# A log-sum-exp over rows whose input is laid out in three pieces instead of two

## The chip, the cores and the metric

The kernel runs on one core of a Trainium2 chip. The metric is the device time of one execution in microseconds, as the median of several runs; a profile of one execution shows the span from its first to its last instruction.

## The reference

```
def setup_inputs():
    batch, seq, dim = 32, 512, 1024
    return {"x": np.random.randn(batch, seq, dim).astype(np.float32)}

def reference(x):
    max_x = np.max(x, axis=-1, keepdims=True)
    return (max_x.squeeze(-1) + np.log(np.sum(np.exp(x - max_x), axis=-1))).astype(np.float32)
```

There are 32 x 512 = 16384 rows of 1024 float32 numbers (67.1 MB in), and one number comes out for each row.

## The kernel before

The 16384 rows are spread over 128 partitions, 128 rows to each. The first 128 x 112 rows of the input form one piece, in which each partition owns 112 consecutive rows (448 KB); the last 128 x 16 rows form the second, in which each partition owns 16 (64 KB). A load takes a stretch of columns of one piece: the same stretch for all partitions, so its 128 parts lie one partition's share apart in memory.

The list LOADS gives 18 loads in order, each with its size in rows and what is done with it. All are issued by SP (L139) into a ring of 48 rows in SBUF. A load is placed behind the one before; if it does not fit ahead of the ring's end, it begins at the ring's start again. Before SP issues a load it waits for every engine step that still reads the ring rows the load will overwrite (the list `users`), and only for these.

The kernel computes exp without subtracting the maximum first, then sums, then takes the Ln. ACT does the exponentials in place (L228) as soon as a load has landed, in the order of the list. The letters say who does the sums:

- R: DVE sums whole rows (L239), so many rows in one instruction.
- F: POOL adds the second half of each row to the first (L233), and DVE sums the halves later (`reduce_folded`, L171). DVE does this behind the next R or T group, or ahead of the next F group.
- T: DVE folds and sums one row with one instruction (L249).
- Y and Z: the last row in two parts, which ACT itself sums (L202).

If a load ends inside a row, ACT also exponentiates the part that has landed. The T rows and the last one are in the small loads at the end, whose sizes fall from 4.46875 rows to 0.46875. When 119 rows are summed, ACT takes the Ln of all rows of the first piece (L268) and SP stores them (L276). At the end ACT takes the Ln of the other 16 rows (L279, L281) and SP stores them (L285). Beside this, DVE and PE check that no sum left the range in which exp without the maximum is safe (L146 to L308); a branch that redoes the work with the maximum follows if the check fails, and is not taken with this input. SP issues load 0 ahead of the start barrier (`start_early`).

The lines that fix the layout and the sizes are:

```
LOADS = [
    (16, "R16"), (16, "R16"), (16, "R16"), (16, "F9 R7"), (13.5, "F6 R7"), (12.5, "R7 F6"),
    (9, "R5 F4"), (7, "F4 R3"), (6, "F2 F2 R2"), (4.46875, "T4"), (3.25, "T3"), (2.46875, "T3"),
    (1.8125, "T2"), (1.3125, "T1"), (0.96875, "T1"), (0.71875, "T1"), (0.53125, "Y"), (0.46875, "Z"),
]
```

Of the kernel before, what the change touches and what calls it, by code (L numbers as in the profile page):

```python
# [13 lines left out]
CEILING = 27.0  # L14
STEEP = 2.0**48
RING = 48
B = 16
LATE = 119

LOADS = [
# [3 lines left out]
]  # L27

# [24 lines left out]
def kernel(  # L53
# [5 lines left out]
    nc = tc.nc  # L59
# [4 lines left out]
    P = nc.NUM_PARTITIONS  # L64
# [6 lines left out]
    x_flat = x.flatten_outer_dims()  # L71
    n, d = x_flat.shape
    assert n % P == 0
    NC = n // P
    H = d // 2
    W = NC - B
    LAST = NC - 1
    x_rows = x_flat[0 : P * W].rearrange("(p c) d -> p (c d)", p=P)
    x_rest = x_flat[P * W : n].rearrange("(p c) d -> p (c d)", p=P)
    out_flat = out.rearrange("a b -> (a b)")  # L80
    out_rows = out_flat[0 : P * W].rearrange("(p c) -> p c", p=P)
    out_rest = out_flat[P * W : n].rearrange("(p c) -> p c", p=P)

    def source(e0, size):
        assert e0 >= W * d or e0 + size <= W * d
        return x_rest[:, e0 - W * d : e0 - W * d + size] if e0 >= W * d else x_rows[:, e0 : e0 + size]

    loads = [
        (int(size * d), [(op[0], 0 if op[0] == "Y" else int(op[1:] or 1)) for op in ops.split()])
# [5 lines left out]
    def sbuf(name, cols, dtype=fp32, rows=P):  # L95
        return nc.alloc_sbuf_tensor(name, [rows, cols], dtype).ap()
# [3 lines left out]
    res = sbuf("res", NC)  # L100
# [18 lines left out]
    sp = Counted(nc, nc.sync, "early_store")  # L119
    done = nc.alloc_semaphore("done")  # L120
    again = nc.alloc_semaphore("again")
    ready = nc.alloc_semaphore("ready")
    stored = nc.alloc_semaphore("stored")
# [10 lines left out]
    def load(i, here, done_before, size):  # L134
        for a, b, who, at in users:
            if a < here + size and b > here:
                sp.wait(who, at)
        users[:] = [u for u in users if not (u[0] < here + size and u[1] > here)]
        return nc.sync.dma_start(  # L139
            out=ring[:, here : here + size], in_=source(done_before, size)  # L140
        ).then_inc(landed[i], 16)
# [36 lines left out]
    c = 0  # L178
    p = 0
# [6 lines left out]
    for i, (size, ops) in enumerate(loads):  # L186
        if here + size > RING * d:
            assert here == p
            p = here = 0
# [7 lines left out]
        for k, (how, s) in enumerate(ops):  # L197
            rows = ring[:, p : p + s * d].rearrange("p (c d) -> p c d", d=d)
            if how in "YZ":
# [3 lines left out]
                    out=last_exp[:, here - p : end - p], in_=ring[:, here:end], func=AF.Exp,  # L203
# [10 lines left out]
            elif how == "A":  # L214
# [3 lines left out]
                    out=v, in_=v, func=AF.Exp, accum_out=sumexp[:, c : c + 1]  # L218
# [11 lines left out]
            if how == "F":  # L230
# [3 lines left out]
                    out=rows[:, :, 0:H], in0=rows[:, :, 0:H], in1=rows[:, :, H:d], op=ALU.add  # L234
                ))
                folded.append((c, s, p, at))
            elif how == "R":
                dve.wait(act, at)
                who = (dve, dve.did(nc.vector.reduce_sum(  # L239
                    out=sumexp[:, c : c + s], in_=rows, axis=AX.X  # L240
                )))
                users.append((p, p + s * d, *who))
            elif how == "T":
# [3 lines left out]
                for r in range(s):  # L247
                    lo = rows[:, r, 0:H]
                    who = (dve, dve.did(nc.vector.scalar_tensor_tensor(  # L249
                        out=lo, in0=lo, scalar=1.0, in1=rows[:, r, H:d],  # L250
# [13 lines left out]
            if c == LATE:  # L264
# [4 lines left out]
                    out=res[:, 0:W], in_=sumexp[:, 0:W], func=AF.Ln  # L269
# [3 lines left out]
                early_act = summed_by_act  # L273
        assert here == end
    sp.wait(act, ln_early)
    nc.sync.dma_start(out=out_rows, in_=res[:, 0:W]).then_inc(sp.sem, 16)  # L276

    act.wait(dve, dve.n)
    act.did(nc.scalar.activation(out=res[:, W:LAST], in_=sumexp[:, W:LAST], func=AF.Ln))  # L279
# [2 lines left out]
        out=res[:, LAST:NC], in_=last_sum, func=AF.Ln, bias=sumexp[:, LAST:NC]  # L282
    ))
    sp.wait(act, ln_last)
    nc.sync.dma_start(out=out_rest, in_=res[:, W:NC]).then_inc(stored, 16)  # L285

# [4 lines left out]
        out=clamped[:, LATE:NC], in0=sumexp[:, LATE:NC], scalar=LOW,  # L291
# [10 lines left out]
        out=over[:, 0:half], in0=last_piece[:, 0:half], scalar=CEILING,  # L302
# [15 lines left out]
            read.then_inc(done, 1)  # L318
    with nc.If(all_fine < 1):

        nc.scalar.wait_ge(sp.sem, 16)
        nc.scalar.wait_ge(stored, 16)
        rows = 0
        steps = 0
        for c0 in range(0, NC, RING):
            s = min(RING, NC - c0)
            v = ring[:, 0 : s * d].rearrange("p (c d) -> p c d", d=d)
            neg = clamped[:, c0 : c0 + s]
            if c0:
                nc.scalar.wait_ge(ready, steps)  # L330
            edge = max(c0, min(W, c0 + s))
            for c1, c2 in ((c0, edge), (edge, c0 + s)):
                if c1 == c2:
                    continue
                nc.scalar.dma_start(
                    out=ring[:, (c1 - c0) * d : (c2 - c0) * d],
                    in_=source(c1 * d, (c2 - c1) * d),
                ).then_inc(again, 16)
                rows += 16
            nc.vector.wait_ge(again, rows)  # L340
            nc.vector.tensor_reduce(
                out=neg, in_=v, op=ALU.max, axis=AX.X, negate=True
            ).then_inc(ready, 1)
            nc.vector.wait_ge(ready, steps + 1)
            nc.vector.tensor_add(
                out=v, in0=v, in1=neg[:, :, None].to_broadcast([P, s, d])
            ).then_inc(ready, 1)
            nc.scalar.wait_ge(ready, steps + 2)
            nc.scalar.activation(out=v, in_=v, func=AF.Exp).then_inc(ready, 1)
            nc.vector.wait_ge(ready, steps + 3)  # L350
            nc.vector.reduce_sum(
                out=sumexp[:, c0 : c0 + s], in_=v, axis=AX.X
            ).then_inc(ready, 1)
            steps += 4
        nc.scalar.wait_ge(ready, steps)
        nc.scalar.activation(out=res, in_=sumexp[:, 0:NC], func=AF.Ln).then_inc(ready, 1)
        nc.vector.wait_ge(ready, steps + 1)
        nc.vector.tensor_sub(out=res, in0=res, in1=clamped).then_inc(ready, 1)
        nc.scalar.wait_ge(ready, steps + 2)
        nc.scalar.dma_start(out=out_rest, in_=res[:, W:NC]).then_inc(again, 16)  # L360
        nc.scalar.dma_start(out=out_rows, in_=res[:, 0:W]).then_inc(again, 16)
        nc.scalar.wait_ge(again, rows + 32)

    nc.scalar.sem_inc(done, 1)
    nc.sync.wait_ge(done, 2)
    nc.sync.wait_ge(sp.sem, 16)
    nc.sync.sem_clear(range(landed[0].num, stored.num))
    kind = dict(sync_type="semaphore", id=stored.num, ant_name="stored")
    nc.sync.add_instruction(mybir.InstEventSemaphore(
# [53 lines left out]
```

## Time and profile before

| | us |
|---|---|
| median of 3 runs | 161.56 (161.54 to 161.56) |
| span of the profiled execution | 160.4 |
| median of the runs less that span | 1.2 |
| ACT busy, DVE busy, POOL busy | 114.5, 114.3, 37.3 |
| input moved, mean rate | 67.1 MB, 419 GB/s |

No time of the profiled execution is listed beside its span; the times of the three runs are of other executions. The busy times are sums over the whole span. A load's time "to landing" counts from its issue by SP to the moment when all its parts are there, and it includes the time for which it lies in the queue behind earlier loads. In the timeline, a bracket at the end of a row gives the idle time ahead of the instruction and what ended it.

### The profile page before, as it was taken

Reading aid. Unit: us, or ns where it says so; the run is one execution under the profiler, and the core shown is the slowest. Engines: PE = TensorE matmul, PEld = TensorE weight load, DVE = VectorE, ACT = ScalarE, POOL = GpSimd, SP = SyncE. Lnnn points to the kernel's source line nnn. Section 1 sums busy time; section 2 is a strip of 40 time slices with the busy share of each in tenths; the row PEclk is TensorE's granted clock in tenths of the full one; section 3 lists DMA queues with packets and bytes.
Section 4 is the critical chain, followed back from the end, with each engine's and each line's share of the span. In section 5 each row is a group of like instructions: output and inputs, shape, how many; then the busy total and the mean of one; then the engine's idle time right before and its main releaser. Section 6 shows DMA issues by size and latency. Waiting matters only on the chain.

```text
span 160.4 us, 219 instructions
## 1 busy us (share of the span) xinstructions
PE 2.2 (1%) x26; PEld 1.1 (1%) x26; DVE 114.3 (71%) x59; ACT 114.5 (71%) x31; POOL 37.3 (23%) x11
## 2 busy tenths in 40 slices
PE   0000000000000000000000000000000000000022
PEld 0000000000000000000000000000000000000011
DVE  0000000009999499994999859959999999999996
ACT  3000059990699708995099949991999989799996
POOL 0000000000000000000000994690004969891000
DMA  7996996996996996996999999999999999999992
GB/s 262 523 523 262 523 523 262 523 507 278 523 490 294 523 490 294 523 490 294 482 441 441 441 425 409 409 409 480 432 395 417 450 416 398 448 411 424 412 413 95
DMA packets 2881, 67.18 MB, mean 419 GB/s; under 512 B 576, under 2 KB 704, under 8 KB 1344
## 3 DMA queue, kind: packets, MB, share of 16 engines
q1 hardware_dynamic: 2880, 67.18, 97.7%
q14 instruction: 1, 0.01, 0.0%
HBM read 67.11 MB, written 0.07 MB: 419 GB/s over the span
## 4 chain that ended last, share of the span: by engine, by line
DMA 52%; ACT 28%; DVE 19%; issue 1%; PE 0%
DMA ring<-in_x_dram 52%; ACT ring L228 27%; DVE sumexp L239 15%; DVE sumexp L171 2%; DVE ring L249 1%; DVE over L301 0%; PE count L306 0%; ACT res L268 0%; DVE clamped L290 0%; DVE fine L308 0%; DVE sumexp L212 0%
## 5 line engine op out<-in xcount | busy, mean ns | idle before, releaser
L228 ACT ACTIVATE ring<-ring 128x16384 f32<-128x16384 f32 (+16 forms) x23 | 111.7, 4908 | 43.0 <-DMA ring<-in_x_dram 43.0
L239 DVE TENSOR_REDUCE sumexp<-ring 128x16 f32<-128x16384 f32 (+4 forms) x9 | 85.6, 9513 | 42.7 <-ACT ring L228 42.7
L233 POOL TENSOR_TENSOR ring<-ring 128x3072 f32<-128x3072 f32 (+3 forms) x7 | 37.1, 5313 | 107.3 <-ACT ring L228 107.3
L171 DVE TENSOR_REDUCE sumexp<-ring 128x6 f32<-128x3072 f32 (+3 forms) x7 | 18.4, 2656 | 0.0
L249 DVE SCALAR_TENSOR_TENSOR ring<-ring 128x512 f32<-128x512 f32 x15 | 9.6, 687 | 0.4 <-ACT ring L228 0.4
L125 ACT ACT_TABLE_LOAD x1 | 1.3, 1283 | 1.4 <-PEq L62 1.4
L156 PE MATMUL count<-far,bad 128*1 128x1 f32 x2 | 0.2, 164 | 153.2 <-DVE clamped L151 153.2
L160 PE MATMUL count<-sumexp,ones 128*1 128x1 f32 x18 | 1.6, 164 | 3.6 <-DVE ring L249 3.6
L249 DVE DVE_READ_ACCUMULATOR ring<-ring 128x1 f32 x15 | 1.2, 82 | 0.0
L202 ACT ACTIVATE last_exp<-ring 128x544 f32<-128x544 f32 (+1 forms) x2 | 1.2, 584 | 0.0
L126 DVE MEMSET ones<- 128x1 f32 x1 | 0.1, 59 | 1.5 <-PEq L62 1.5
L156 PEld LDWEIGHTS count<-far,bad 128*1 128x1 f32 x2 | 0.1, 80 | 153.2 <-DVE clamped L151 153.2
L160 PEld LDWEIGHTS count<-sumexp,ones 128*1 128x1 f32 x18 | 0.8, 80 | 4.5 <-DVE ring L249 4.5
L301 DVE SCALAR_TENSOR_TENSOR over<-ring 128x240 f32<-128x240 f32 x1 | 0.4, 404 | 0.0
L308 DVE TENSOR_SCALAR fine<-count 1x1 int32<-1x1 f32 x1 | 0.1, 147 | 0.3 <-PE count L306 0.3
L151 DVE SCALAR_TENSOR_TENSOR clamped<-clamped,sumexp 128x119 f32<-128x119 f32 x1 | 0.3, 283 | 0.0
L268 ACT ACTIVATE res<-sumexp 128x112 f32<-128x112 f32 x1 | 0.3, 279 | 0.0
L281 ACT ACTIVATE res<-last_sum,sumexp 128x1 f32<-128x1 f32 x1 | 0.3, 261 | 0.0
L202 ACT ACTIVATION_READ_ACCUMULATOR last_exp<-ring 128x1 f32 x2 | 0.3, 126 | 0.0
L146 DVE TENSOR_SCALAR clamped<-sumexp 128x119 f32<-128x119 f32 x1 | 0.2, 221 | 0.0
L279 ACT ACTIVATE res<-sumexp 128x15 f32<-128x15 f32 x1 | 0.2, 209 | 0.0
L290 DVE SCALAR_TENSOR_TENSOR clamped<-sumexp 128x9 f32<-128x9 f32 x1 | 0.2, 169 | 0.0
(17 smaller groups left out, 1.8 us busy)
## 6 DMA issues: line engine op xcount, KB each, us to landing
ring<-in_x_dram SPq DMA_DIRECT2D x1, 6912.0 KB, 23.9
ring<-in_x_dram SPq DMA_DIRECT2D x1, 6400.0 KB, 19.7
ring<-in_x_dram SPq DMA_DIRECT2D x1, 4608.0 KB, 15.9
ring<-in_x_dram SPq DMA_DIRECT2D x1, 3584.0 KB, 24.0
ring<-in_x_dram SPq DMA_DIRECT2D x1, 3072.0 KB, 19.1
ring<-in_x_dram SPq DMA_DIRECT2D x1, 2288.0 KB, 24.1
ring<-in_x_dram SPq DMA_DIRECT2D x1, 1664.0 KB, 20.9
ring<-in_x_dram SPq DMA_DIRECT2D x1, 1264.0 KB, 23.6
```

Of the source, the lines that this page charges most:

```text
L125: nc.scalar.preload_act_table_set("natural_log_exp_and_others")
L151: dve.did(nc.vector.scalar_tensor_tensor(out=clamped[:, 0:LATE], in0=clamped[:, 0:LATE], scalar=0.0, in1=sumexp[:, 0:LATE], op0=ALU.bypass ...
L156: pe.did(nc.tensor.matmul(count, lhsT=bad[:, 0:1], rhs=far, start=True, stop=False))
L160: return pe.did(nc.tensor.matmul(count, lhsT=ones, rhs=sumexp[:, c : c + 1], **kw))
L171: at = dve.did(nc.vector.reduce_sum(out=sumexp[:, c0 : c0 + s0], in_=halves, axis=AX.X))
L202: at = act.did(nc.scalar.activation(out=last_exp[:, here - p : end - p], in_=ring[:, here:end], func=AF.Exp, accum_out=first_sum if how == ...
L228: at = act.did(nc.scalar.activation(out=v, in_=v, func=AF.Exp))
L233: at = pool.did(nc.gpsimd.tensor_tensor(out=rows[:, :, 0:H], in0=rows[:, :, 0:H], in1=rows[:, :, H:d], op=ALU.add))
L239: who = (dve, dve.did(nc.vector.reduce_sum(out=sumexp[:, c : c + s], in_=rows, axis=AX.X)))
L249: who = (dve, dve.did(nc.vector.scalar_tensor_tensor(out=lo, in0=lo, scalar=1.0, in1=rows[:, r, H:d], op0=ALU.mult, op1=ALU.add, accum_out ...
L268: ln_early = act.did(nc.scalar.activation(out=res[:, 0:W], in_=sumexp[:, 0:W], func=AF.Ln))
L301: dve.did(nc.vector.scalar_tensor_tensor(out=over[:, 0:half], in0=last_piece[:, 0:half], scalar=CEILING, in1=last_piece[:, half : 2 * half ...
```

## The change

The input is cut into three pieces instead of two: the first 128 x 15 rows, with 15 consecutive rows (60 KB) to a partition; the next 128 x 96, with 96 (384 KB); and the last 128 x 17, with 17 (68 KB). A load may not cross from one piece into the next, so the sizes change with the pieces: load 0 has 15 rows and takes the whole first piece, load 3 has 15 (F8 R7 for F9 R7), load 4 has 14.5 (F6 R8 for F6 R7), and load 9 has 5.46875 (T5 for T4). All other loads keep their sizes. The early store becomes two stores, one for each of the first two pieces, and the last store holds 17 rows to a partition instead of 16. The waits on the early stores' semaphore count to 32 instead of 16.

```diff
-B = 16
+A = 15
+B = 17
...
-    (16, "R16"), (16, "R16"), (16, "R16"), (16, "F9 R7"), (13.5, "F6 R7"), (12.5, "R7 F6"),
-    (9, "R5 F4"), (7, "F4 R3"), (6, "F2 F2 R2"), (4.46875, "T4"), (3.25, "T3"), (2.46875, "T3"),
+    (15, "R15"), (16, "R16"), (16, "R16"), (15, "F8 R7"), (14.5, "F6 R8"), (12.5, "R7 F6"),
+    (9, "R5 F4"), (7, "F4 R3"), (6, "F2 F2 R2"), (5.46875, "T5"), (3.25, "T3"), (2.46875, "T3"),
...
-    x_rows = x_flat[0 : P * W].rearrange("(p c) d -> p (c d)", p=P)
-    x_rest = x_flat[P * W : n].rearrange("(p c) d -> p (c d)", p=P)
     out_flat = out.rearrange("a b -> (a b)")
-    out_rows = out_flat[0 : P * W].rearrange("(p c) -> p c", p=P)
-    out_rest = out_flat[P * W : n].rearrange("(p c) -> p c", p=P)
+    parts = [
+        (
+            c0, c1, x_flat[P * c0 : P * c1].rearrange("(p c) d -> p (c d)", p=P),
+            out_flat[P * c0 : P * c1].rearrange("(p c) -> p c", p=P),
+        )
+        for c0, c1 in ((0, A), (A, W), (W, NC))
+    ]
 
     def source(e0, size):
-        assert e0 >= W * d or e0 + size <= W * d
-        return x_rest[:, e0 - W * d : e0 - W * d + size] if e0 >= W * d else x_rows[:, e0 : e0 + size]
+        (piece,) = [
+            rows[:, e0 - c0 * d : e0 - c0 * d + size] for c0, c1, rows, _ in parts
+            if c0 * d <= e0 and e0 + size <= c1 * d
+        ]
+        return piece
...
     sp.wait(act, ln_early)
-    nc.sync.dma_start(out=out_rows, in_=res[:, 0:W]).then_inc(sp.sem, 16)
+    for c0, c1, _, to in parts[:2]:
+        nc.sync.dma_start(out=to, in_=res[:, c0:c1]).then_inc(sp.sem, 16)
...
-    nc.sync.dma_start(out=out_rest, in_=res[:, W:NC]).then_inc(stored, 16)
+    nc.sync.dma_start(out=parts[2][3], in_=res[:, W:NC]).then_inc(stored, 16)
...
-    nc.sync.wait_ge(sp.sem, 16)
+    nc.sync.wait_ge(sp.sem, 32)
```

More of the change, by code (lines that the diff above doesn't have):

```diff
@@ L319 @@
     with nc.If(all_fine < 1):
-        nc.scalar.wait_ge(sp.sem, 16)
+        nc.scalar.wait_ge(sp.sem, 32)
         nc.scalar.wait_ge(stored, 16)
@@ L330 @@
                 nc.scalar.wait_ge(ready, steps)
-            edge = max(c0, min(W, c0 + s))
-            for c1, c2 in ((c0, edge), (edge, c0 + s)):
-                if c1 == c2:
+            for c1, c2, _, _ in parts:
+                c1, c2 = max(c0, c1), min(c0 + s, c2)
+                if c1 >= c2:
                     continue
@@ L359 @@
         nc.scalar.wait_ge(ready, steps + 2)
-        nc.scalar.dma_start(out=out_rest, in_=res[:, W:NC]).then_inc(again, 16)
-        nc.scalar.dma_start(out=out_rows, in_=res[:, 0:W]).then_inc(again, 16)
-        nc.scalar.wait_ge(again, rows + 32)
+        for c0, c1, _, to in parts:
+            nc.scalar.dma_start(out=to, in_=res[:, c0:c1]).then_inc(again, 16)
+        nc.scalar.wait_ge(again, rows + 48)
     nc.scalar.sem_inc(done, 1)
     nc.sync.wait_ge(done, 2)
-    nc.sync.wait_ge(sp.sem, 16)
+    nc.sync.wait_ge(sp.sem, 32)
     nc.sync.sem_clear(range(landed[0].num, stored.num))
```

## The prediction

> **What bounds the kernel now.** I read the page first: engines, DMA row, queues and the chain that ended last.
>
> ```profile
> span 160.4 us, 219 instructions
> PE 2.2 (1%) x26; PEld 1.1 (1%) x26; DVE 114.3 (71%) x59; ACT 114.5 (71%) x31; POOL 37.3 (23%) x11
> q1 hardware_dynamic: 2880, 67.18, 97.7%
> DMA 52%; ACT 28%; DVE 19%; issue 1%; PE 0%
> ```
>
> The queue that brings the input is busy for 97.7% of the span, while ACT and DVE work for 71% each. The bytes do not change, so the stream can gain only at its start or from a better rate; it can lose by running dry. But the kernel ends when the last exponentials are done, so the next view is the chain of waits in order of time, from 130 us on, followed by the timeline of ACT and of SP's queue in narrow windows.
>
> ```profile
> 119.11 19.09 DMA ring<-in_x_dram
> 138.20 0.02 issue
> 138.22 12.34 ACT ring L228 x5
> 150.56 0.18 ACT res L268
> 150.75 6.06 ACT ring L228 x4
> ...
> 143.65 6.91 ACT L228 ACTIVATE ring<-ring 128x4576 f32<-128x4576 f32 x2
> 150.66 2.29 ACT L228 ACTIVATE ring<-ring 128x2528 f32<-128x2528 f32 x1
> ...
> 158.01 0.56 ACT L202 ACTIVATE last_exp<-ring 128x480 f32<-128x480 f32 x1
> 158.67 0.26 ACT L281 ACTIVATE res<-last_sum,sumexp 128x1 f32<-128x1 f32 x1
> ...
> 158.95 0.34 SPq L285 DMA_DIRECT2D out_dram<-res  x1
> 119.48 0.43 SPq L139 DMA_DIRECT2D ring<-in_x_dram  x1
> ```
>
> I count loads from 0. The load of 4.46875 rows is load 9: SP issued it at 119.48. Its landing comes from the page's list of DMA issues (size, median us from issue to landing), with others that I need later:
>
> ```profile
> ring<-in_x_dram SPq DMA_DIRECT2D x1, 4608.0 KB, 15.9
> ring<-in_x_dram SPq DMA_DIRECT2D x1, 3584.0 KB, 24.0
> ring<-in_x_dram SPq DMA_DIRECT2D x1, 3072.0 KB, 19.1
> ring<-in_x_dram SPq DMA_DIRECT2D x1, 2288.0 KB, 24.1
> out_dram<-res SPq DMA_DIRECT2D x1, 56.0 KB, 7.4
> out_dram<-res SPq DMA_DIRECT2D x1, 8.0 KB, 1.4
> ```
>
> 119.48 + 24.1 = 143.6, and ACT begins that load at 143.65. From 138.22 ACT has no gap to the end, yet it is not behind the stream either: load 9 is begun as it lands, and so is each later one, because the exponentials of one load take about as long as the next load's transfer. The kernel is bound by the stream and by ACT at once, with next to no slack between them. Then come the last Ln, the store issued at 158.95 and its 1.4 us, which end the span at 160.4.
>
> **The tail: ACT's share of load 9.** Cumulative rows after each load are 16, 32, 48, 64, 77.5, 90, 99, 106, 112, 116.47 before; after, 15, 31, 47, 62, 76.5, 89, 98, 105, 111, 116.47. So the first nine landings come a row (load 3: two) earlier, but load 9 lands after the same bytes as before and carries one row more (T5 for T4, 5600 columns for 4576). The loads behind it are unchanged. The price of that row on ACT is from the groups by form:
>
> ```profile
> L228 ACT ACTIVATE ring<-ring 128x16384 f32<-128x16384 f32 x3 | 41.6, 13857 | 30.2 <-DMA ring<-in_x_dram 30.2
> L228 ACT ACTIVATE ring<-ring 128x6144 f32<-128x6144 f32 x2 | 10.6, 5314 | 2.4 <-DMA ring<-in_x_dram 2.4
> ```
>
> (13857 - 5314) / 10240 = 0.834 ns a column, so 1024 columns cost 0.85 us. The row was taken from ahead of load 9, where ACT had waited for data anyway, and put where ACT does not wait. ACT starts load 9 at 143.65 as before and is 0.85 us late from there on. Nothing gives that back: every later load is already begun at its landing, with ACT's pieces as long as the transfers. DVE adds a fifth fold of load 9:
>
> ```profile
> L249 DVE SCALAR_TENSOR_TENSOR ring<-ring 128x512 f32<-128x512 f32 x15 | 9.6, 687 | 0.4 <-ACT ring L228 0.4
> 147.70 0.69 DVE L249 SCALAR_TENSOR_TENSOR ring<-ring 128x512 f32<-128x512 f32 x1
> 150.16 0.09 DVE L249 DVE_READ_ACCUMULATOR ring<-ring 128x1 f32 x1
> ```
>
> With their overlap about 0.61 us each (load 9's four take from 147.70 to 150.2 in the timeline); 0.35 us of it fills the idle time shown, the other 0.26 is hidden by DVE's waits for ACT at loads 14 and 15; if that cover were gone it would cost that 0.26. Term one: **+0.85 us**.
>
> **The ring: what load 7 now waits for.** The ring holds 48 rows and wraps at load 3 and load 6. Before, load 7 took ring rows 9 to 16, where load 3's R7 had been; its data was free with load 6's. After, load 3 is 15 rows long (F8 R7), so ring rows 9 to 16 overlap load 4's F6 group (ring rows 15 to 21). Load 7 must now wait for DVE's sum of that folded group (L171), which before only load 8 waited for. Rows of the timeline, DVE, ACT, POOL and SP:
>
> ```profile
> 41.33 13.86 ACT L228 ACTIVATE ring<-ring 128x16384 f32<-128x16384 f32 x1 [5.46 <-DMA ring<-in_x_dram]
> 60.68 13.86 ACT L228 ACTIVATE ring<-ring 128x16384 f32<-128x16384 f32 x1 [5.49 <-DMA ring<-in_x_dram]
> 74.57 17.22 DVE L239 TENSOR_REDUCE sumexp<-ring 128x16 f32<-128x16384 f32 x1 [2.13 <-ACT ring L228]
> 80.02 13.95 ACT L228 ACTIVATE ring<-ring 128x9216 f32<-128x9216 f32 x2 [5.49 <-DMA ring<-in_x_dram]
> 94.00 7.62 DVE L239 TENSOR_REDUCE sumexp<-ring 128x7 f32<-128x7168 f32 x1 [2.22 <-ACT ring L228]
> 96.36 11.82 ACT L228 ACTIVATE ring<-ring 128x6144 f32<-128x6144 f32 x2 [2.39 <-DMA ring<-in_x_dram]
> 101.54 4.94 DVE L171 TENSOR_REDUCE sumexp<-ring 128x9 f32<-128x4608 f32 x1
> 101.76 6.71 POOL L233 TENSOR_TENSOR ring<-ring 128x3072 f32<-128x3072 f32 x1 [3.80 <-ACT ring L228]
> 106.51 0.81 SPq L139 DMA_DIRECT2D ring<-in_x_dram  x2
> 108.21 7.62 DVE L239 TENSOR_REDUCE sumexp<-ring 128x7 f32<-128x7168 f32 x1 [1.73 <-ACT ring L228]
> 115.74 3.34 DVE L171 TENSOR_REDUCE sumexp<-ring 128x6 f32<-128x3072 f32 x1
> 119.11 0.33 SPq L139 DMA_DIRECT2D ring<-in_x_dram  x1
> 0.00 139.24 SPq L139 DMA_DIRECT2D ring<-in_x_dram  x18
> 22.00 13.86 ACT L228 ACTIVATE ring<-ring 128x16384 f32<-128x16384 f32 x1 [19.27 <-DMA ring<-in_x_dram]
> ```
>
> A row of input takes (60.68 - 41.33) / 16 = 1.21 us. DVE takes (17.22 - 7.62) / 9 rows = 1.07 us a row. After the change, load 4 (F6 R8) is begun by ACT at 96.36 - 1.21 = 95.15 and, at 11.82 + 0.85, done at 107.82; DVE sums R8 from 107.85 for 7.62 + 1.07 = 8.69 to 116.54, then the folded six (begun 0.09 before, as in the rows) to 119.79. DVE is free in time: load 2's sum ends at 91.79 - 1.21 = 90.58; load 3's data lands two rows earlier, ACT ends it at 77.60 + 13.10 = 90.70, and its R7 and F8 sums end near 102.7. POOL's fold ends near 107.2. So SP issues load 7 at about 119.8, against 106.9 before.
>
> When does the queue need it? Load 6 landed at 106.51 + 15.9 = 122.4; one row earlier that is 121.2. Load 7 took 130.9 - 122.4 = 8.5 us of transfer (issue 106.9 + 24.0). An uninterrupted stream lands it at 129.7. A load issued into a queue that runs dry has its start cost in view. No such load stands in this trace but load 0: issued at 0.0, landed at 22.0, of which 19.35 is the transfer of 16 rows, so 2.65 us beside the transfer; load 7 would land at 119.8 + 2.65 + 8.5 = 130.95, 1.25 us late. The other bound is the final 8 KB store, 1.4 us in all: 129.7, nothing lost. A gain is excluded, as the bytes ahead of load 7 are the same whenever it comes. I take 0.85, two thirds of the way to load 0's end: load 0 is the like transfer, a large load into an idle queue, but it starts while the program is in its start barrier. Behind load 7 on SP are loads 8 and 9, issued within a microsecond of it and not needed for 8 us; what is lost is passed to load 9, to ACT and to the end. Term two: **+0.85 us**, bounds 0 and 1.25.
>
> The Trainium skill (DMA: Bandwidth & Descriptors, "Anatomy of one DMA", fitted there for transfers issued from GpSimd) states a fixed cost of about 2.0 us per DMA; with it, as an estimate, load 7 lands 0.6 us late and the total is 163.0. The trace's two rows, 2.65 and 1.4, lie on either side of it.
>
> **The rest.** The first load being contiguous, at 60 KB a partition instead of a 448 KB step, could shorten load 0's 2.65 us: between 0 and 1.25 (down to the store's 1.4). I take 0: of two steps in this trace, 448 KB (loads 1 to 8) and 64 KB (loads 9 on), both stream alike: load 9's 4.47 rows took 143.6 - 138.2 = 5.4 us, 1.21 a row. For the same reason the 384 KB step of the middle and the 68 KB of the last piece are costed at 0. One store of 56 KB becomes two; SP issues the second 0.35 us later, near 152, and they lie in the queue behind the last load (the 56 KB took 7.4 us, to 158.2); the final store at 158.95 covers both. Without that cover it would be 0.35. The final store's pieces are 68 bytes for 64, its Ln 16 columns for 15: nothing. The other waits of SP for ring rows (loads 3, 4, 5, 6 and 10) move earlier or by under a microsecond, with several in hand: load 5 is issued at 90.6, load 4 lands only at 95.1.
>
> **Sum.** Span 160.4 + 0.85 + 0.85 = 162.1. The median of the three runs is 161.56, 1.16 above the span; that part is kept: 161.56 + 1.70 = **163.3 us**.
>
> **Rivals.**
> - *The refill is hidden.* Load 7's start cost is near the store's 1.4. Only ACT's row is left: 161.56 + 0.85 = 162.4. For it, the queue is warm; against it, load 0's 2.65. Chance 0.25.
> - *The start was slowed by the 448 KB step (faster).* If load 0's 2.65 us comes from 16 streams stepping alike through memory, the contiguous load starts like the store, the whole stream moves 1.25 earlier, and load 7's refill is cheap too: 161.56 + 0.85 - 1.25 = 161.2. It decides from the point where the start gains over 0.85 us more than the refill loses. Against it: loads 1 to 8 show no such loss in the same step. Chance 0.09; a start that gains about 0.85 alone (no change) 0.04.
> - *The 384 KB step is slower.* The loads in the middle then take longer, each row of 96. If a row cost 0.04 us more, the stream would end 3.8 us later, at about 166.2 with ACT's row. Against it: 448 and 64 KB stream alike. Chance 0.03. The Trainium skill (same page, "Latency and other measured facts") has a 512 KiB step at 207 GB/s where 214 is full; no step here is a power of two but the 64 KB of the last rows, which the trace shows at full rate.
>
> **How the numbers follow.** Forecast case (ACT's row and a dry queue), 163.3, own range 162.7 to 163.8, chance 0.59. Some 0.2% (0.3 us) is what a measurement of this kernel tells from no change. Slower by more than that: 0.59 + 0.25 + 0.03 = 0.87; same 0.04; faster 0.09. The range from 162.0 (hidden refill with a somewhat better start) to 164.0 (1.25 for the refill, 0.3 for the rest) leaves out the faster, the unchanged and the slow-step case, 0.16.
>
> **What would show it.** Right: SP issues the 3584 KB load near 119.8 after a wait for the six-row sum, and it lands near 130.5, some 11 us after issue instead of 24.0; the GB/s row dips near 121; ACT starts the 5600 columns as they land, near 144.5, and the next load's exponentials begin 0.85 us after that load's landing. Wrong: load 0 lands well before 20.8 (22.0 less a row), which is the faster rival; the spacing of landings in the middle over 1.21 us a row; or load 7 landing at 129.7, which leaves 162.4.

## The result, and the profile after

The changed kernel takes 163.98 us (median of 4 runs, 163.92 to 164.03) against 161.56 for the kernel before: a ratio of 1.0146, 95% interval 1.0132 to 1.016. The forecast was 163.3 with a range of 162.0 to 164.0. The profiled execution has a span of 162.4 us and took 163.94, so 1.5 us lie outside its span.

The page after, in the lines that answer to those shown of before:

```profile
span 162.4 us, 223 instructions
PE 2.2 (1%) x26; PEld 1.1 (1%) x26; DVE 114.0 (70%) x61; ACT 114.4 (70%) x31; POOL 36.2 (22%) x11
q1 hardware_dynamic: 3024, 67.18, 97.0%
DMA 53%; DVE 25%; ACT 19%; SPq 0%; issue 0%; PE 0%
```

Busy times and bytes hardly moved. What is new is small: SPq, SP's issuing, is in the chain, and DVE has taken some of ACT's share. The chain in order of time shows where (start us, us, what):

```profile
95.52 12.68 ACT ring L235 x2
...
108.22 8.69 DVE sumexp L246
116.90 3.27 DVE sumexp L178
120.17 0.02 issue
120.19 0.33 SPq L146
...
121.04 23.81 DMA ring<-in_x_dram
144.84 0.02 issue
144.87 4.88 ACT ring L235
149.75 0.02 issue
149.77 5.00 DVE ring L256 x16
```

The chain now runs through the sum of R8, the sum of the folded six rows, and SP's issue of loads 7 to 9 right behind it. The page's list of issues (size, us to landing) and the timeline of SP and ACT give the landings:

```profile
ring<-in_x_dram SPq DMA_DIRECT2D x1, 3584.0 KB, 10.7
ring<-in_x_dram SPq DMA_DIRECT2D x1, 3072.0 KB, 17.7
ring<-in_x_dram SPq DMA_DIRECT2D x1, 2800.0 KB, 23.8
out_dram<-res SPq DMA_DIRECT2D x1, 8.5 KB, 1.4
...
120.19 0.33 SPq L146 DMA_DIRECT2D ring<-in_x_dram  x1
144.87 4.87 ACT L235 ACTIVATE ring<-ring 128x5600 f32<-128x5600 f32 x1 [1.12 <-DMA ring<-in_x_dram]
149.64 2.96 ACT L235 ACTIVATE ring<-ring 128x3328 f32<-128x3328 f32 x1
159.97 0.56 ACT L209 ACTIVATE last_exp<-ring 128x480 f32<-128x480 f32 x1
160.91 0.33 SPq L293 DMA_DIRECT2D out_dram<-res  x1
```

Load 7 (3584 KB) is issued at 120.19 and lands 10.7 us later, at 130.9, where it used to lie in the queue for most of 24.0. Whether the queue was empty meanwhile is seen in narrow windows (us, busy times and counts by engine, granted TensorE clock, DMA share, GB/s):

```profile
119.00:120.00 1.00, 0.00 (x0) 0.00 (x0) 1.00 (x1) 1.00 (x1) 0.00 (x0) 1.00 0.85 369
120.00:121.00 1.00, 0.00 (x0) 0.00 (x0) 1.00 (x2) 1.00 (x1) 0.00 (x0) 1.00 0.01 0
121.00:122.00 1.00, 0.00 (x0) 0.00 (x0) 1.00 (x1) 1.00 (x2) 0.31 (x1) 1.00 1.71 459
```

Between 120 and 121 the DMA engines start nothing. (The 1.71 behind it shows that these windows count a packet where it begins; what had begun before 120 still ran into the hole. Load 6 itself lands only at 121.5, 18.4 us after its issue at 103.14. So these windows show the hole but not its price, which e3 below gives.) Load 9 is begun by ACT at 144.87 instead of 143.65, 1.22 later. Its exponentials take 4.87 instead of 4.02, and the last piece's begin at 159.97 instead of 158.01, 1.96 later. The final store is 1.96 later too.

### The profile page after: what moved, and what is told of

Read it like the earlier page. It is cut to its first block, busy times and chain, and to the rows that moved or that the text cites. A ratio compares the mean times of both kernels' runs of the same rounds, so it can differ in the third digit from the quotient of the medians.

```text
span 162.4 us, 223 instructions
## 1 busy us (share of the span) xinstructions
PE 2.2 (1%) x26; PEld 1.1 (1%) x26; DVE 114.0 (70%) x61; ACT 114.4 (70%) x31; POOL 36.2 (22%) x11
## 4 chain that ended last, share of the span: by engine, by line
DMA 53%; DVE 25%; ACT 19%; SPq 0%; issue 0%; PE 0%
DMA ring<-in_x_dram 53%; ACT ring L235 19%; DVE sumexp L246 16%; DVE ring L256 6%; DVE sumexp L178 2%; SPq L146 0%; DVE over L309 0%; DVE clamped L158 0%; DVE clamped L153 0%; PE count L314 0%; DVE clamped L298 0%; DVE fine L316 0%; DVE sumexp L219 0%
## 5 line engine op out<-in xcount | busy, mean ns | idle before, releaser
L235 ACT ACTIVATE ring<-ring 128x2048 f32<-128x2048 f32 (+17 forms) x23 | 111.7, 4906 | 45.0 <-DMA ring<-in_x_dram 45.0
L246 DVE TENSOR_REDUCE sumexp<-ring 128x16 f32<-128x16384 f32 (+6 forms) x9 | 85.5, 9511 | 44.0 <-ACT ring L235 44.0
L240 POOL TENSOR_TENSOR ring<-ring 128x3072 f32<-128x3072 f32 (+3 forms) x7 | 36.0, 5155 | 108.4 <-ACT ring L235 108.4
L178 DVE TENSOR_REDUCE sumexp<-ring 128x6 f32<-128x3072 f32 (+3 forms) x7 | 17.9, 2581 | 0.0
## 6 DMA issues: line engine op xcount, KB each, us to landing
ring<-in_x_dram SPq DMA_DIRECT2D x1, 4608.0 KB, 18.4
ring<-in_x_dram SPq DMA_DIRECT2D x1, 3584.0 KB, 10.7
ring<-in_x_dram SPq DMA_DIRECT2D x1, 1664.0 KB, 21.1
```

What stands on the lines that cost most here:

```text
L178: at = dve.did(nc.vector.reduce_sum(out=sumexp[:, c0 : c0 + s0], in_=halves, axis=AX.X))
L235: at = act.did(nc.scalar.activation(out=v, in_=v, func=AF.Exp))
L240: at = pool.did(nc.gpsimd.tensor_tensor(out=rows[:, :, 0:H], in0=rows[:, :, 0:H], in1=rows[:, :, H:d], op=ALU.add))
L246: who = (dve, dve.did(nc.vector.reduce_sum(out=sumexp[:, c : c + s], in_=rows, axis=AX.X)))
```

## The experiments

All runs of before that these were compared with had a median of 161.6 to 161.7. Spans below are means over each kernel's runs; "outside" is time less span, again a mean.

| kernel | median us | ratio to before, 95% | span | outside |
|---|---|---|---|---|
| before (15, 21 and 27 runs) | 161.69, 161.68, 161.59 | | 160.3 to 160.4 | 1.32 to 1.35 |
| changed (4 runs) | 163.98 | 1.0132 to 1.016 | 162.4 | 1.58 |
| e1 layout only | 161.94 | 1.0006 to 1.0024 | 160.4 | 1.53 |
| e2 sizes only | 163.81 | 1.0113 to 1.0144 | 162.5 | 1.34 |
| e3 swap | 163.00 | 1.007 to 1.0097 | 161.5 | 1.54 |
| e4 cut | 163.72 | 1.0109 to 1.014 | 162.0 | 1.71 |
| e5 store split | 161.65 | 0.999 to 1.0008 | 160.3 | 1.34 |
| e6 swap and cut | 162.82 | 1.0056 to 1.0083 | 161.1 | 1.70 |
| e7 17 loads | 162.04 | 1.0015 to 1.0033 | 160.7 | 1.41 |
| e8 long branch | 161.85 | 1.0004 to 1.0022 | 160.3 | 1.53 |
| e9 layout, short branch | 161.69 | 0.9996 to 1.0014 | 160.3 | 1.35 |
| e10 empty branch | 161.74 | 0.9991 to 1.0009 | 160.3 | 1.33 |

**Layout or sizes.** e1 takes the three pieces and three stores, and keeps the old sizes:

```diff
-A = 15
-B = 17
+A = 16
+B = 16
...
-    (15, "R15"), ... (15, "F8 R7"), (14.5, "F6 R8"), ... (5.46875, "T5"),
+    (16, "R16"), ... (16, "F9 R7"), (13.5, "F6 R7"), ... (4.46875, "T4"),
```

> Three pieces (16, 96 and 16 rows to a partition) and three stores, but all load sizes, the ring and the T4 load as before. Theory (the sizes cost the time: load 7's wait in a dry queue and one more row for ACT in load 9): within 0.3 us of before, 161.3 to 161.9; load 7 lands near 130.9, load 9 near 143.6. Rival (the layout costs it: a slower start of the contiguous load, a slower 384 KB step, one store more): 0.4 us slower or more, with load 0 landing after 22.0 or over 1.21 us a row in the middle, or a time further above the span than before.

e2 takes the new sizes on two pieces (111 and 17 rows to a partition), with one early store:

```diff
-        for c0, c1 in ((0, A), (A, W), (W, NC))
+        for c0, c1 in ((0, W), (W, NC))
...
```

> Two pieces (111 and 17 rows to a partition) and two stores, with the changed kernel's load sizes. Theory: nearly all of the loss, 163.3 to 164.0; SP issues load 7 at 119.8 to 120.2 after the six-row sum and it lands 10.7 us later; load 9's exponentials start near 144.5. Rival (layout): back to 161.6 to 162.4.

The sizes carry the loss: e2 has all of the 2 us of span, e1 next to none of it (160.4). At 161.94, e1 is 0.04 above the band of the theory and well under the 0.4 us of the rival. But its 0.25 us lie mostly outside the span, which is a place that the rival had named. Its timeline shows the start and the 384 KB step to be neutral:

```profile
22.07 13.86 ACT L235 ACTIVATE ring<-ring 128x16384 f32<-128x16384 f32 x1 [19.34 <-DMA ring<-in_x_dram]
41.41 13.86 ACT L235 ACTIVATE ring<-ring 128x16384 f32<-128x16384 f32 x1 [5.48 <-DMA ring<-in_x_dram]
60.74 13.86 ACT L235 ACTIVATE ring<-ring 128x16384 f32<-128x16384 f32 x1 [5.48 <-DMA ring<-in_x_dram]
```

A contiguous first load of 16 rows lands as late as before (22.07 against 22.00), and the next 16 rows at the new step take 19.33 us against 19.35.

**The dry queue.** e3 makes load 7 wait for R8 instead of the folded six, by one swap in the list:

```diff
-    (14.5, "F6 R8"),
+    (14.5, "R8 F6"),
```

> The changed kernel with load 4 worked as R8 F6 instead of F6 R8, so that load 7 waits for the sum of R8 only, some 8 us earlier. Theory: the queue no longer runs dry, load 7 lands 8.5 us after load 6, and 0.9 to 1.25 us of the loss go: 162.7 to 163.1; ACT's row in load 9 (0.85) is left. Rival (the queue had not run dry in a way that counts, the loss is the layout's or ACT's): 163.7 to 164.0.

It took 163.00, 0.98 less than the changed kernel (0.9 of span), within what the theory gave. The same windows of e3, and its rows for load 7 and load 9:

```profile
119.00:120.00 1.00, 0.00 (x0) 0.00 (x0) 1.00 (x1) 1.00 (x1) 0.00 (x0) 1.00 1.02 442
120.00:121.00 1.00, 0.00 (x0) 0.00 (x0) 1.00 (x1) 1.00 (x1) 0.00 (x0) 1.00 1.07 459
121.00:122.00 1.00, 0.00 (x0) 0.00 (x0) 1.00 (x1) 1.00 (x2) 0.41 (x1) 1.00 1.07 459
...
111.57 0.81 SPq L146 DMA_DIRECT2D ring<-in_x_dram  x2
143.91 4.87 ACT L235 ACTIVATE ring<-ring 128x5600 f32<-128x5600 f32 x1 [1.12 <-DMA ring<-in_x_dram]
```

Load 7 is issued at 111.57, the hole is gone, and ACT begins load 9 at 143.91, 0.96 earlier than in the changed kernel. Some 0.1 of this was there before the hole, as ACT began load 5 at 110.55 in e3 and at 110.65 in the changed kernel. So the wait costs about 0.9 us. e2 has the old layout and the same wait: its load 7 is issued at 120.05 and takes 11.0 us to land.

**ACT's extra row.** e4 cuts load 9 so that ACT can take the extra row while the rest is under way:

```diff
-    (5.46875, "T5"),
+    (1, "T1"), (4.46875, "T4"),
```

> The changed kernel with load 9 cut in two, 1 row (T1) and 4.46875 rows (T4), so that ACT can take the extra row before the rest has landed; one DMA more. Theory: ACT's 0.85 goes, less some 0.1 for the added instruction: 163.1 to 163.3. Rival (DVE's fifth fold or the stores hold the end, not ACT's row): 163.8 to 164.0.

The time missed the forecast of the theory (163.72, not 163.1 to 163.3). The trace shows the mechanism right and the mending costlier than allowed for:

```profile
145.03 4.02 ACT L235 ACTIVATE ring<-ring 128x4576 f32<-128x4576 f32 x1 [0.24 <-DMA ring<-in_x_dram]
...
159.41 0.57 ACT L209 ACTIVATE last_exp<-ring 128x480 f32<-128x480 f32 x1
160.37 0.33 SPq L293 DMA_DIRECT2D out_dram<-res  x1
```

ACT again does 4576 columns as they land, and the final store is issued 0.54 earlier (160.37 for 160.91), though load 9's last part is 0.16 later with one DMA more. But the span ended only 0.4 earlier, as that store took 1.6 us to its end instead of 1.4, and 0.13 went outside the span. Why that store takes longer here and in e6 is not shown.

**Both.** e6 has both edits.

> The changed kernel with both mendings, load 4 as R8 F6 and load 9 cut into 1 and 4.46875 rows. Theory (refill and ACT's row are separate terms): the refill's 0.9 to 1.0 and the cut's 0.4 of span both go, span 160.8 to 161.1, time 162.5 to 162.8. Rival (they overlap): 162.9 to 163.2.

It gave 162.82, 0.02 above the theory's band and under the rival's, with a span of 161.1: 1.3 below the changed kernel's, the sum of 0.9 and 0.4. The two terms are separate. What is left against before is 0.7 of span and 0.36 outside it. In the profiled execution the final store is issued 0.30 later than before (159.25 for 158.95) and takes 1.6 us instead of 1.4.

**The time outside the span.** Five kernels (e5 and e7 to e10) ask what adds 0.2 us there. e5 splits the early store of the kernel before:

```diff
-    nc.sync.dma_start(out=out_rows, in_=res[:, 0:W]).then_inc(sp.sem, 16)
+    for c0, c1 in ((0, W // 2), (W // 2, W)):
+        nc.sync.dma_start(out=out_rows[:, c0:c1], in_=res[:, c0:c1]).then_inc(sp.sem, 16)
...
```

> The kernel before with its early store (112 columns) issued as two of 56 columns; all else as before. Open: three stores went with 0.25 us more of device time at an unchanged span. Theory (each DMA more adds time outside the span): span 160.3 to 160.5, time 161.85 to 162.0, so 1.5 above the span instead of 1.3. Rival (it is the layout, not the number of DMAs): 161.6 to 161.75.

No effect: one store more costs nothing there. e7 has one load less:

```diff
-    (4.46875, "T4"), (3.25, "T3"), (2.46875, "T3"), (1.8125, "T2"), (1.3125, "T1"),
-    (0.96875, "T1"), (0.71875, "T1"), (0.53125, "Y"), (0.46875, "Z"),
+    (4.5, "T4"), (3.375, "T3"), (2.5, "T3"), (1.875, "T2"), (1.375, "T1"),
+    (1.0625, "T1"), (0.75, "T1 Y"), (0.5625, "Z"),
```

> The kernel before with its last nine loads made into eight (4.5, 3.375, 2.5, 1.875, 1.375, 1.0625, 0.75 and 0.5625 rows), one DMA less. Theory (each DMA costs about 0.2 outside the span): time 1.1 above the span; the coarser tail costs 0.1 to 0.3 of span, so 161.5 to 161.8. Rival (the number of DMAs does not matter): 161.8 to 162.0.

It misses both bands: 0.3 us slower in the span with its coarser tail, and nothing won outside (1.41 for 1.34). The remaining difference was the branch that is not taken: with three pieces, its copies and stores are more instructions. e8 adds such instructions to the kernel before, and e9 takes them from e1:

```diff
-            for c1, c2 in ((c0, edge), (edge, c0 + s)):
+            mid = (c0 + edge) // 2
+            for c1, c2 in ((c0, mid), (mid, edge), (edge, c0 + s)):
...
-        nc.scalar.dma_start(out=out_rows, in_=res[:, 0:W]).then_inc(again, 16)
+        nc.scalar.dma_start(out=out_rows[:, 0 : W // 2], in_=res[:, 0 : W // 2]).then_inc(again, 16)
+        nc.scalar.dma_start(out=out_rows[:, W // 2 : W], in_=res[:, W // 2 : W]).then_inc(again, 16)
...
```

> The kernel before with four more DMA instructions in the branch that is not taken (its copies and one of its stores cut in two); what runs is the same. Open: 0.2 us of the loss lie outside the span and go with the three-piece kernels, not with the third store. Theory (the length of the program, the untaken branch included, costs it): span 160.3 to 160.4, time 161.85 to 162.1. Rival (the strides in memory cost it): 161.6 to 161.75.

```diff
-            for c1, c2, _, _ in parts:
+            for c1, c2, _, _ in parts[1:]:
...
-        for c0, c1, _, to in parts:
+        for c0, c1, _, to in parts[1:]:
             nc.scalar.dma_start(out=to, in_=res[:, c0:c1]).then_inc(again, 16)
...
```

> The three-piece layout of the first experiment with the branch that is not taken cut back to the number of DMAs that it had before (its copies leave out the first piece). Theory (length of the program): 161.6 to 161.75, 1.3 above the span. Rival (strides in memory): 161.85 to 162.05, as in the first experiment.

> The kernel before without the work of the branch that is not taken (the redoing with the maximum is left out). Theory (length of the program): faster than before by 0.2 us or more, at an unchanged span. Rival: 161.6 to 161.75.

e8 executes what before executes, at the same span, and is 0.2 us slower (1.53 outside for 1.34). e9 has the layout of e1 without the longer branch, and is back at 1.35. So the layout's 0.2 us is the longer untaken branch. It is no price per instruction: two DMAs more in that branch (e1) cost as much as four (e8), and e10, with that branch empty, wins nothing. What sets the step is not shown. Nor is what puts e4 and e6, with one load more, at 1.7 outside the span, a further 0.15.

## Why the prediction was right, and where it was off

*The wait of load 7.* Right in its place and mechanism. The time of issue was forecast as 119.8 and was 120.19. The reason is a step that was not priced: load 0, shorter by a row, was taken to land 1.21 us earlier, at 20.8, and in the changed kernel's timeline ACT began it later:

```profile
21.14 13.00 ACT L235 ACTIVATE ring<-ring 128x15360 f32<-128x15360 f32 x1 [18.40 <-DMA ring<-in_x_dram]
40.47 13.86 ACT L235 ACTIVATE ring<-ring 128x16384 f32<-128x16384 f32 x1 [6.33 <-DMA ring<-in_x_dram]
59.82 13.86 ACT L235 ACTIVATE ring<-ring 128x16384 f32<-128x16384 f32 x1 [5.50 <-DMA ring<-in_x_dram]
```

Only 0.86 was won at load 0, and the 0.35 that is missing runs through to load 4 (95.52, not 95.15). In e2, on two pieces, load 0 was begun at 21.00, 0.2 later than the forecast, so the shorter first load wins less than a row's time there too; why, the runs do not settle.

*The refill.* The start cost was bounded by 1.4 and 2.65 and taken as 2.25, a choice within wide bounds. Measured: 10.7 less 8.5 of transfer, 2.2; e4 (10.8) and e2 (11.0) give 2.3 and 2.5. The Trainium skill's 2.0 (DMA: Bandwidth & Descriptors, "Anatomy of one DMA") is 0.2 to 0.5 lower. With the issue at 120.19, load 7 landed at 130.9 instead of 129.7 and passed it all to load 9: 1.22 us where the term said 0.85. From ACT's begin of load 5 to its begin of load 7 the changed kernel takes 20.31 us (110.65 to 130.96) and e3 19.43 (110.55 to 129.98), so the hole itself cost 0.88 (0.95 in e4, 1.12 in e2), near the 0.85 forecast. The other 0.35 is the gain that is missing at the start.

*ACT's row.* 4.87 less 4.02 is 0.85, as forecast. The sign given for it is there too: load 10 (1664 KB), issued at 127.72, landed 21.1 us later at 148.8, and ACT began it at 149.64, some 0.8 late. "Nothing gives that back" was a little too strong: of 1.22 + 0.85 = 2.07, 1.96 reached the end. DVE's fifth fold cost nothing on the path of the result, but only just: DVE worked without a break from 149.77 and had its last sum ready at 160.31, and the last two Ln follow ACT, from 160.52 on. The chain names DVE in the tail, but what follows it there, the check, ends ahead of the final store's 1.4 us.

*The part outside the span.* It was kept at 1.16 and was 1.58 as a mean. This step of the sum was wrong: a term of 0.2 us was missing, of a branch that never runs (e8, e9). The rest of the difference is in the 1.16 itself, which set one execution's span against the median of others; 1.32 to 1.35 is what the runs of before show when each is set against its own span.

*How close it was.* The time is 0.68 above the forecast: 0.26 of it in the span (1.96 for 1.70) and 0.42 outside. It lies above the forecast case's own range (to 163.8) and only 0.02 under the upper end of the whole range. That end was made of a dearer refill and 0.3 for the rest; no part of it was worked out for the two things that were missed, the start and the part outside the span. The mechanism was right, but that the range held was luck.

*The rivals.* The hidden refill (162.4) fell with the empty window. The faster start fell in e1: the contiguous first load starts no sooner. The slow 384 KB step fell with the same rows, 19.33 us for 16 rows. At the step of the last rows, 68 KB for 64, nothing shows either: ACT began load 8 at 138.24 and load 9 at 144.87, each as it landed, which is 6.63 us for 5.47 rows, again 1.21 a row. e2, with 444 KB for 384, has the changed kernel's span.

## What to carry to other kernels

When a list of load sizes is shifted against a ring, work out anew which load waits for which reader: one row moved a load's wait from a buffer long free to the last sum of a group, and the stream lost 0.9 us. Order the work on a load so that the part whose buffer is wanted first is summed first; that was one swap in the list. Where each load's work fits just under the next load's transfer, a row added to one load is paid nearly in full. To carry a time over from a span, take both from the same execution.

## What the runs showed of the hardware

- A load of 3584 KB, issued when the queue had nothing left to start, took 2.2 to 2.5 us from issue to landing beside its transfer (changed kernel, e4, e2), against 2.65 for load 0 at the program's start and 1.4 for the whole of the small final store.
- Four DMA instructions added to a branch that is not taken cost 0.2 us of device time at an unchanged span (e8: 1.53 outside it for 1.34); emptying the branch won nothing (e10: 1.33).
- ACT began a first load of 60 KB a partition at 21.00 to 21.14 (five kernels) and one of 64 KB at 21.86 to 22.07 (seven kernels): 0.7 to 1.1 us apart, where the rate of the stream says 1.21.
- Steps of 64, 68, 384, 444 and 448 KB from partition to partition showed no difference in rate: 19.33 to 19.35 us for 16 rows at the three large ones, 1.21 us a row at the two small ones.
